# A two-layer diffusion block: low weight parts moved to VectorE, stages of the second attention layer dealt over two cycles, weight splits pinned

## The chip, the cores and the metric

The kernel runs on one core of one Trainium2 chip. The metric is the time of one execution on the device, in microseconds (us). Several executions are timed, and one more is recorded by the profiler, which gives the start and length of every instruction on TensorE (PE for its matmuls, PEld for its weight loads), VectorE (DVE), ScalarE (ACT), GpSimd (POOL) and SyncE (SP, which here only issues DMAs).

## The reference

Two trunk layers over 512 latent tokens and 256 context tokens, width 1024, in float32. Layer 0 mixes tokens by differential attention (8 heads, two maps of 64 channels each, QK-norm, rotary embedding), layer 1 by neighbourhood attention (16 heads, a learned position bias in a window, plus all context tokens). Each mixer is followed by an MLP with 4096 hidden units. Cut to what matters:

```python
for i in range(2):
    h_l = modulate(rms_norm(x, norm1_g[i]), mod_l[0], mod_l[1])
    h_c = modulate(rms_norm(ctx, norm1_g[i]), mod_c[0], mod_c[1])
    # layer 0: softmax(q0 k0) - lam * softmax(q1 k1), times v; rms_norm; times w_o
    # layer 1: softmax([q k_window + bias, q k_ctx]) times v; times w_o
    y_l, y_c = mixer(h_l, h_c, ...)
    x = x + mod_l[2] * y_l
    x = x + mod_l[5] * squared_relu_mlp(modulate(rms_norm(x, norm2_g[i]), ...), w_mlp1[i], w_mlp2[i])
    # the same for ctx in layer 0; layer 1 needs the latent tokens alone
return x
```

## The kernel before

Every float32 operand of a large matmul is split into a high part (rounded by a copy on ACT) and a low part (the operand minus the high part, a subtraction on DVE or POOL), and a product is three passes: high by high, high by low, low by high. So each weight piece needs a DMA into one of two raw buffers (tile R, line 129, `wraw`), a copy on ACT (line 145) and a subtraction (line 146, both in `wsplit`). A raw buffer is free again when both have read it. In the MLPs and in layer 0's attention the subtraction is on POOL; in layer 1's attention it is on DVE, because `split` passes `eng=nc.vector`.

Each attention layer is a software pipeline over heads (layer 0, 8 of them) or pairs of heads (layer 1, 8 groups), written out as a list of words that `run` executes in order. A word is a kind and a number; a prime means the head before the current one, two primes the one before that:

- `w`k issues the DMA of weight piece k of the next head, `c`k splits it. Four pieces make a head.
- `Q`i`a`, `Q`i`b` are the two halves (over the contraction) of the projection of token tile i to q, k and v; in layer 1 `Qi` of tiles 0 and 1 (context, no q) is one step. After the last half the accumulator (PSUM tag A) is emptied: raw q and k into a Y tile (line 412), v into its high and low parts (465 and 466 in layer 0, 619 and 620 in layer 1), squares and their sums (416, 418), a power on POOL (293), and in layer 0 the rotation (470 to 480), on POOL except for three tiles of head 0.
- `U`i transposes two tiles of q and k (496 in layer 0; 633 and 635 in layer 1) and splits them (430 to 447).
- `S`i are scores and softmax (514 to 526; 655 to 669), `T`i transposes the probabilities and splits them (538 to 541; 685 to 687), `V`i multiplies by v (549; 700) and `O`i transposes the output (566).
- `m` and `n` are pieces of the modulation, `x`, `X`, `P`, `B` belong to the output projection: fetch a head's output from DRAM (737), split it (742, 743), one half of one tile of the projection (749), and the start with weight piece 3 and the gates.

`CYCLE0`, `START0` and `END0` are layer 0's lists, `CYCLE1`, `LAST1` and `END1` layer 1's. In these stretches PE, SP and POOL keep the order in which the instructions are emitted (`PINNED`). ACT and DVE do not: at build time a scheduler with its own estimate of times sorts their instructions, so a split whose DMA it takes as landed can stand ahead of work that was emitted earlier. On the chip each engine then runs its own list strictly in order.

PSUM banks set further order. In layer 1, `PS_ATTN1` gives three banks for A, three for scores (S) and two for B, which T (two of them) and V (one) share. In layer 0, `PS_ATTN0` gives one bank for transposes (C), two for B, two for A and one set of three for scores. Of SBUF tiles, Y has six buffers, E (probabilities), X and R two, N four; H has eight, four for each group in layer 1.

## Time and profile before

| | |
|---|---|
| median of 3 runs | 1918.09 us (1917.07 to 1920.08) |
| the profiled execution's own time | 1917.39 us |
| its span | 1915.6 us |
| PE busy | 1796.2 us, 94% of the span |
| DVE, ACT, POOL busy | 1132.3, 834.9, 808.8 us |
| granted TensorE clock over the span | 0.979 |

The span is the stretch from the first to the last instruction that the profiler recorded; the time of the execution holds a little more. Busy time is the union of an engine's instructions. The granted clock is the share of full TensorE speed that the chip allowed: below 1.00 the same matmuls take longer. In a row of the timeline the columns are start, length, engine, line, operation, the tile written and the tiles read, shapes and count; square brackets hold the time for which the engine had stood idle before, and what ended that. In a row of waits stand who waited, for whom, the total, the number of times and the longest.

### The profile page before, as it was taken

The page shows a single profiled execution, that of the slowest core. Times are in us where ns is not written, and L with a number is a line of the kernel's source. Part 1 is how long each engine was busy: PE and PEld are TensorE (multiplying, and loading weights), DVE is VectorE, ACT ScalarE, POOL GpSimd, SP SyncE. Part 2 cuts the span into 40 slices and gives each one's busy share as a digit, 9 for nine tenths or more (in the row PEclk, how much of TensorE's full clock was granted, in tenths as well). Part 3 has the DMA queues.
Part 4 walks back from the last instruction along what each step waited for, and adds up shares of the span by engine and source line. Part 5 has one row for each costly group of instructions (what it writes and reads, how often), then busy time and mean ns, then how long its engine had stood idle before and what let it go on. Part 6 is the DMA issues. An engine that isn't in the chain of part 4 may idle for free.

```text
span 1915.6 us, 27143 instructions
## 1 busy us (share of the span) xinstructions
PE 1796.2 (94%) x10256; PEld 1572.7 (82%) x10256; DVE 1132.3 (59%) x2158; ACT 834.9 (44%) x1854; POOL 808.8 (42%) x688
## 2 busy tenths in 40 slices
PE   6789999997999999999999998998997989999998
PEld 5777888885789888888888978898887878888886
DVE  4478877887664343343344686777676664444447
ACT  4476666675342212212221245666677342232321
POOL 3555565653333424333342533333345444344443
PEclk9899999998999999999999999999998999999999
DMA  8122212225324443443441232112202323223332
GB/s 326 35 89 79 68 65 84 86 86 189 115 73 146 138 139 126 150 165 110 165 153 46 67 106 71 56 59 77 86 29 88 116 81 105 90 88 100 99 99 77
DMA packets 66499, 197.61 MB, mean 103 GB/s; under 512 B 8192, under 2 KB 23488, under 8 KB 60224
## 3 DMA queue, kind: packets, MB, share of 16 engines
q1 hardware_dynamic: 58608, 186.03, 29.4%
q10 hardware_dynamic: 7760, 9.85, 1.5%
q8 instruction: 80, 1.31, 0.3%
q14 instruction: 51, 0.42, 0.1%
HBM read 180.74 MB, written 15.11 MB: 102 GB/s over the span
## 4 chain that ended last, share of the span: by engine, by line
PE 71%; DVE 12%; ACT 5%; DMA 5%; issue 4%; POOL 3%; ACTq 0%; SPq 0%; POOLq 0%; DVEq 0%
PE PD L829 22%; PE PA L405 11%; PE PA L864 11%; PE PB L864 9%; PE PA L749 4%; PE PB L700 2%; PE PA L254 2%; PE PS L514 2%; PE PB L549 1%; DMA R<-in_wqa_dram 1%; DMA R<-in_wqb_dram 1%; PE PS L655 1%; ACT E L520 1%; PE PQ L395 1%; ACT W L145 1%
## 5 line engine op out<-in xcount | busy, mean ns | idle before, releaser
L146 POOL TENSOR_TENSOR W<-R,W 128x1024 fp32r<-128x1024 f32 x142 | 351.4, 2485 | 541.2 <-ACT W L145 541.1
L829 PE MATMUL PD<-Q,W 128*128 128x384 f32 (+2 forms) x1992 | 395.8, 345 | 2.4 <-DVE Q L331 1.1
L145 ACT ACTIVATE W<-R 128x1024 fp32r<-128x1024 f32 (+1 forms) x172 | 172.4, 1021 | 462.3 <-PE PA L864 193.5
L829 PEld LDWEIGHTS PD<-Q,W 128*128 128x128 f32 x1992 | 345.2, 188 | 34.0 <-issue 8.6
L864 PE MATMUL PA<-W,H 128*128 128x512 f32 x1080 | 275.5, 394 | 4.6 <-POOL W L146 2.9
L864 PEld LDWEIGHTS PA<-W,H 128*128 128x128 f32 x1080 | 200.2, 188 | 51.5 <-issue 4.5
L838 DVE TENSOR_TENSOR N<-N 128x768 f32<-128x768 f32 (+1 forms) x64 | 67.0, 1048 | 278.8 <-ACT N L834 170.3
L864 PE MATMUL PB<-W,H 128*128 128x512 f32 x840 | 209.3, 391 | 0.0
L864 PEld LDWEIGHTS PB<-W,H 128*128 128x128 f32 x840 | 157.4, 188 | 33.3
L405 PE MATMUL PA<-W,Q 128*128 128x384 f32 (+1 forms) x1008 | 172.4, 323 | 4.2 <-DVE H L620 3.8
L405 PEld LDWEIGHTS PA<-W,Q 128*128 128x128 f32 x1008 | 157.1, 189 | 6.1 <-DVE H L620 5.5
L293 POOL TENSOR_TENSOR SQ<-SQ,half 128x4 f32<-128x4 f32 (+1 forms) x96 | 93.9, 979 | 132.6 <-DVE SQ L418 131.7
L405 PE MATMUL PA<-WB,H 128*128 128x384 f32 x576 | 110.5, 344 | 9.9 <-DVE Q L466 9.9
L841 DVE SCALAR_TENSOR_TENSOR H<-N,H 128x768 fp32r<-128x768 f32 (+1 forms) x64 | 98.1, 1533 | 25.7 <-ACT H L840 25.0
L405 PEld LDWEIGHTS PA<-WB,H 128*128 128x128 f32 x576 | 100.5, 191 | 11.0 <-DVE Q L466 10.5
L749 PE MATMUL PA<-W,H 128*128 128x512 f32 x384 | 98.6, 409 | 5.6 <-POOL H L743 3.1
L829 PE MATMUL PD<-H,W 128*128 128x512 f32 (+1 forms) x408 | 94.4, 379 | 2.5 <-DVE SA L287 2.0
L875 DVE TENSOR_TENSOR H<-PA,H 128x512 f32<-128x512 f32 x78 | 53.9, 690 | 69.6 <-PE PA L864 69.6
L749 PEld LDWEIGHTS PA<-W,H 128*128 128x128 f32 x384 | 73.3, 196 | 23.9 <-POOL H L743 3.9
L829 PEld LDWEIGHTS PD<-H,W 128*128 128x128 f32 x408 | 74.0, 189 | 18.0 <-DVE H L331 2.9
L514 PE MATMUL PS<-Q,Q 128*128 128x256 f32 (+1 forms) x320 | 68.6, 346 | 18.3 <-ACT E L520 10.0
L520 ACT ACTIVATE E<-PS,SA 128x768 f32<-128x768 f32 (+1 forms) x96 | 72.7, 758 | 27.9 <-DVE SA L519 25.5
(208 smaller groups left out, 3064.4 us busy)
## 6 DMA issues: line engine op xcount, KB each, us to landing
R<-in_w_dram SPq DMA_DIRECT2D x128, 512.0 KB
M<-in_wmod_dram SPq DMA_DIRECT2D x48, 1024.0 KB
R<-in_wqa_dram SPq DMA_DIRECT2D x32, 384.0 KB
R<-in_wqb_dram SPq DMA_DIRECT2D x32, 384.0 KB
Y<-in_rpb_dram SPq DMA_DIRECT2D x48, 128.0 KB
bias<-Y SPq DMA_DIRECT2D x48, 128.0 KB
X<-bias SPq DMA_DIRECT2D x8, 768.0 KB
R<-in_woa_dram SPq DMA_DIRECT2D x8, 512.0 KB
```

The costliest lines, as they stand in the source:

```text
L145: nc.scalar.activation(w[:, 0, :n], raw, AF.Copy)
L146: low = (eng or nc.gpsimd).tensor_sub(w[:, 1, :n], raw, w[:, 0, :n].bitcast(F32))
L293: nc.gpsimd.tensor_tensor(r, ss, self.half[:, :n], op=ALU.pow)
L405: nc.tensor.matmul(acc[:, :n], hT[kt][:, x, P * i:P * i + P], w[kt // 2][:, y, o:o + n], start=(kt == 0 and p == 0), stop=(kt == KT - 1 an ...
L514: nc.tensor.matmul(s[:, c0:c1], q[:, m, P * i:P * i + P], k[:, m, c0:c1], start=p == 0, stop=p == 1)
L520: nc.scalar.activation(e[:, m, :nk], s, AF.Exp, bias=mx[:, 0:1], accum_out=sm[:, m:m + 1])
L749: nc.tensor.matmul(ps, oHL[h][:, x, c:c + P], w[h // 2][:, y, 512 * (h % 2):512 * (h % 2) + 512], start=(first and h == hs[0] and p == 0), ...
L829: nc.tensor.matmul(ps[:, at:at + b1 - b0], w[kt // 4][:, x, o:o + P], hT[kt][:, y, b0:b1], start=(kt == 0 and p == 0), stop=(kt == KT - 1 ...
L838: nc.vector.tensor_mul(r, r, r)
L841: nc.vector.scalar_tensor_tensor(u[:, 1, :], r, 1.0, u[:, 0, :].bitcast(F32), op0=ALU.mult, op1=ALU.subtract)
L864: nc.tensor.matmul(ps, hd[:, x, P * i - c0:P * i - c0 + P], w[f][:, y, 512 * n:512 * n + 512], start=(f == 0 and p == 0), stop=(f == len(h ...
L875: nc.vector.tensor_add(av, ps, av)
```

## The change

1. In layer 0's attention the subtraction of `wsplit` goes to DVE (`eng=nc.vector`) for heads 2 to 7. Heads 0 and 1 are loaded through other calls and stay on POOL.
2. The copy and the subtraction of the weight splits in both attention layers, and of the split `X` in the output projection, are given to `keep_in_program_order`: at build time each is tied behind the instruction that was emitted just before it on its engine, so the scheduler can't sort it ahead of that.
3. `c3` moves in `CYCLE0` from before `Q2a` to after `V1'`. `END0` deals its `X` and `P` steps out anew.
4. In layer 1, `T3`, `V2` and `V3` of a group move into the cycle after next, among the first steps (`T3''`, `V2''`, `V3''`), `V1` to the end of the next; `Q0` and `Q1` become two halves each; `U0` moves up; `c1 w3` moves down. `LAST1` and `END1` follow.
5. Head 0's second rotation buffer comes from the tag OT (two buffers) and no longer from Y.

```diff
-CYCLE0 = """w0 w1 Q0a O2'' n1' S1' O3'' V4'' V5'' c0 w2 U4' Q0b c1 w3 Q1a T0' T1' Q1b c2 O4'' S2' V0' c3 Q2a O5'' Q2b
-S3' T2' U0 Q3a V1' O0' Q3b S4' T3' Q4a Q4b V2' O1' m0 S5' T4' U2 n0 Q5a V3' Q5b m1 S0 T5'"""
+CYCLE0 = """w0 w1 Q0a O2'' n1' S1' O3'' V4'' V5'' c0 w2 U4' Q0b c1 w3 Q1a T0' T1' Q1b c2 O4'' S2' V0' Q2a O5'' Q2b
+S3' T2' U0 Q3a V1' c3 O0' Q3b S4' T3' Q4a Q4b V2' O1' m0 S5' T4' U2 n0 Q5a V3' Q5b m1 S0 T5'"""
...
-END0 = """x0 x1 x2 x3 S1' O2'' O3'' V4'' T0' U4' n1' V5'' T1' X0 S2' X1 O4'' x4 X2 x5 P0a O5'' V0' S3' X3 T2' X4 B0
-X5 P0b P1a V1' O0' S4' m0 P1b V2' O1' x6 P2a T3' n0 P2b T4' S5' P3a O2' P3b V3' V4' m1 T5' P4a O3' n1 X6
-P4b V5' P5a P5b O4' O5'"""
-CYCLE1 = """w0 w1 Q0 U4' Q1 c0 w2 S0' Q2a S1' c1 w3 Q2b Q3a T0' Q3b S2' T1' Q4a S3' V0' Q4b V1' Q5a c2 T2' Q5b c3 T3'
-V2' U0 U2 V3'"""
-LAST1 = """Q0 U4' Q1 c0 x0 x1 S0' Q2a S1' Q2b X0 x2 Q3a T0' Q3b X1 x3 S2' T1' Q4a S3' V0' X2 Q4b V1' Q5a T2' Q5b T3'
-V2' U0 U2 V3'"""
-END1 = """c1 X3 x4 U4' S0' S1' x5 T0' S2' X4 c2 T1' P2a V0' S3' X5 P3a B0 V1' P4a T2' V2' x6 P2b T3' X6 P3b V3' P4b
-P5a P5b"""
+END0 = """x0 x1 x2 x3 S1' O2'' O3'' V4'' T0' U4' n1' X0 V5'' T1' X1 S2' O4'' X2 x4 V0' S3' x5 P0a O5'' T2' X3 P1a
+X4 V1' O0' S4' X5 B0 P0b m0 V2' O1' x6 P1b T3' n0 P2a T4' S5' P2b O2' P3a V3' V4' P3b m1 T5' P4a O3' n1
+X6 P4b V5' P5a P5b O4' O5'"""
+CYCLE1 = """w0 w1 Q0a T3'' U4' Q1a c0 w2 V2'' V3'' Q0b S0' Q1b Q2a S1' Q2b Q3a T0' S2' Q4a c1 w3 T1' Q3b S3' V0' U0
+Q4b Q5a c2 T2' Q5b c3 U2 V1'"""
+LAST1 = """Q0a T3'' U4' Q1a c0 x0 x1 V2'' V3'' Q0b S0' Q1b X0 x2 Q2a S1' Q2b X1 Q3a T0' S2' Q4a T1' Q3b X2 S3' V0'
+U0 Q4b Q5a T2' Q5b U2 V1'"""
+END1 = """x3 x4 T3'' c1 U4' V2'' V3'' S0' X3 x5 P2a S1' c2 X4 P3a T0' S2' X5 T1' P4a B0 S3' V0' V1' P2b T2' x6 P3b
+T3' V2' X6 P4b V3' P5a P5b"""
...
-    def wsplit(self, raw, n, tile=None, eng=None, tag='W'):
+    def wsplit(self, raw, n, tile=None, eng=None, tag='W', pinned=False):
...
-        nc.scalar.activation(w[:, 0, :n], raw, AF.Copy)
+        high = nc.scalar.activation(w[:, 0, :n], raw, AF.Copy)
         low = (eng or nc.gpsimd).tensor_sub(w[:, 1, :n], raw, w[:, 0, :n].bitcast(F32))
+        if pinned:
+            self.tc.keep_in_program_order(high)
+            self.tc.keep_in_program_order(low)
...
             else:
-                t2 = self.sbt('Y', [P, 2, 2, 64])
+                t2 = self.sbt('OT' if accs else 'Y', [P, 2, 2, 64])
...
-            for hf in (0, 1) if i < 2 else (half,):
-                self.qkv_matmul(acc[i], hf, w, hT, i, c0, 384 - c0)
-            if half == 1 or i < 2:
+            self.qkv_matmul(acc[i], half, w, hT, i, c0, 384 - c0)
+            if half == 1:
...
-            nc.scalar.activation(u[:, 0, :], st, AF.Copy)
-            eng.tensor_sub(u[:, 1, :], st, u[:, 0, :].bitcast(F32))
+            self.tc.keep_in_program_order(nc.scalar.activation(u[:, 0, :], st, AF.Copy))
+            self.tc.keep_in_program_order(eng.tensor_sub(u[:, 1, :], st, u[:, 0, :].bitcast(F32)))
...
-                    w.setdefault(h, []).append(b.wsplit(raws.pop((h, k)), 768, tag=("WA", "WB")[h % 2]))
+                    w.setdefault(h, []).append(b.wsplit(raws.pop((h, k)), 768, eng=nc.vector, tag=("WA", "WB")[h % 2], pinned=True))
...
-                    w.setdefault(g, []).append(b.wsplit(raws.pop((g, k)), 768, eng=nc.vector, tag="W1"))
+                    w.setdefault(g, []).append(b.wsplit(raws.pop((g, k)), 768, eng=nc.vector, tag="W1", pinned=True))
```

## The prediction, before the change was built

> **What bounds it now.** First the page's head, then busy times by stage, then PE's waits in each stage, last the order of instructions around each wait.
>
> ```profile
> span 1915.6 us, 27143 instructions
> PE 1796.2 (94%) x10256; PEld 1572.7 (82%) x10256; DVE 1132.3 (59%) x2158; ACT 834.9 (44%) x1854; POOL 808.8 (42%) x688
> ```
>
> PE is the bound, and 119 us of the span are without it. The windows (columns: length, then busy of PE, PEld, DVE, ACT, POOL, granted clock, DMA share, GB/s) show where the change can reach:
>
> ```profile
> 67.00:205.00 138.00, 118.15 (x749) 104.72 (x750) 104.33 (x250) 88.37 (x259) 78.34 (x98) 0.96 0.20 68
> 205.00:405.00 200.00, 187.76 (x1287) 172.75 (x1286) 159.58 (x370) 137.71 (x395) 118.41 (x151) 1.00 0.24 83
> 405.00:513.00 108.00, 94.63 (x554) 76.71 (x552) 81.54 (x159) 59.48 (x157) 43.65 (x47) 0.95 0.39 137
> 1157.70:1199.40 41.70, 39.59 (x249) 38.65 (x250) 27.07 (x69) 22.77 (x64) 16.15 (x21) 0.96 0.12 39
> 1199.40:1411.10 211.70, 193.42 (x1292) 187.86 (x1291) 151.72 (x351) 143.23 (x350) 74.46 (x91) 0.94 0.19 63
> 1411.10:1453.00 41.90, 37.95 (x265) 36.49 (x264) 29.91 (x71) 30.27 (x74) 20.59 (x22) 1.00 0.18 58
> 1453.00:1506.00 53.00, 42.76 (x234) 37.82 (x233) 30.81 (x67) 32.78 (x73) 26.43 (x23) 0.81 0.35 119
> ```
>
> The rows are START0, four CYCLE0 passes, END0 with its tail, then layer 1's attention in four pieces; the fifth holds five periods of 42.3 us. PE idles 19.9, 12.2, 13.4, 2.1, 18.3, 4.0 and 10.2 us in them. Where the clock is under 1.00, matmuls also run slower: 265 in 37.95 us at clock 1.00 make 143 ns each, so 1292 would be 185.0 us instead of 193.42, a further 8.4 us in the five periods. The rest of the kernel (both MLPs, the handovers) has the same program afterwards.
>
> PE's waits (total, times, longest), first START0, then the CYCLE0 passes, END0, and the five periods of layer 1:
>
> ```profile
> PE PA L405 <- DVE Q L466: 9.9, 2, 8.6
> ...
> PE PB L538 <- DVE E L526: 4.8, 4, 1.6
> PE PS L514 <- ACT E L520: 4.3, 4, 1.3
> PE PS L514 <- ACT Q L443: 2.0, 4, 0.8
> ...
> PE PS L514 <- ACT Q L443: 4.2, 2, 2.6
> PE PA L749 <- POOL H L743: 3.1, 2, 2.2
> ...
> PE PB L700 <- DVE N L687: 13.6, 5, 2.8
> ```
>
> **The low parts and the pins, layer 0.** One pass; the first line is from the chain of waits (start, length), the others from the timeline:
>
> ```profile
> 303.21 3.38 DMA R<-in_wqa_dram
> ...
> 301.35 1.84 POOL L146 TENSOR_TENSOR WA<-R,WA 128x768 fp32r<-128x768 f32 x1
> 306.62 0.84 ACT L145 ACTIVATE WA<-R 128x768 fp32r<-128x768 f32 x1 [1.13 <-DMA R<-in_wqa_dram]
> 307.37 0.88 ACT L520 ACTIVATE E<-PS,SA 128x768 f32<-128x768 f32 x1
> 307.78 1.82 POOL L146 TENSOR_TENSOR WA<-R,WA 128x768 fp32r<-128x768 f32 x1
> 308.39 1.68 PE L514 MATMUL PS<-Q,Q 128*128 128x512 f32 x8 [1.20 <-ACT E L520]
> 308.37 0.17 DVE L523 RECIPROCAL SA<-SA 128x2 f32<-128x2 f32 x1 [2.76 <-ACT E L520]
> 308.77 0.98 DVE L558 SCALAR_TENSOR_TENSOR O<-O,SO,one 128x128 f32<-128x128 f32 x1
> ```
>
> The fourth weight piece of the pass is fetched only when a low part on POOL has freed one of two R buffers (301.35 + 1.84); it takes 3.38 us, and its high part c3 has been sorted ahead of the second exponential on ACT, waits 1.13 us for the DMA, and the exponential and PE wait behind it. The other row to see is L558: 0.98 us while POOL's low part runs (307.78 to 309.60), where L553 of the same shape takes 0.35 on average (below). It sits in front of L526, for which PE waits next.
>
> The change moves 24 low parts (heads 2 to 7, four each) from POOL to DVE:
>
> ```profile
> L146 POOL TENSOR_TENSOR WA<-R,WA x16: 1809/1825/1847, 23.2 to 307.8; 128x768 fp32r<-128x768 f32 x16
> L146 DVE TENSOR_TENSOR W<-R,W x24: 947/958/960, 1157.9 to 1417.6; 128x768 fp32r<-128x768 f32 x24
> L558 DVE SCALAR_TENSOR_TENSOR O<-O,SO,one 128x128 f32<-128x128 f32 x24 | 14.5, 606 | 0.6 <-POOL SO L293 0.3
> L553 DVE SCALAR_TENSOR_TENSOR O<-PB,SA,O 128x128 f32<-128x128 f32 x23 | 8.0, 347 | 3.1 <-ACT O L552 2.6
> ```
>
> POOL loses 24 x 1.83 = 44 us, DVE gains 24 x 0.96 = 23 us. Of those, 14 fall into 205 to 405: 13.4 us, less what L558 no longer loses, 24 x (606 - 347) ns = 6.2 us. DVE goes from 159.6 to about 167 of some 192 us. R is freed about 2 us earlier (POOL reached that low part only after other work, and needs 0.87 us more for it). SP then issues w2 and w3 earlier; nothing else queues between them but the M and oT fetches. c3 moves from before Q2a to after V1': ten steps later, so its DMA of 3.4 us has landed. w3 itself stays; only the next pass's w1 waits for c3's buffer, and that is not asked for until the next pass begins. I expect the 1.20 us before the scores and most of the L526 waits to go: of 11.1 us, I take 8. Bounds: all 12.2 gained, or 13.4 lost if every low part lies on the path.
>
> **START0.** The second buffer of the rotation moves from Y (6 buffers) to OT for head 0.
>
> ```profile
> 82.92 0.38 ACT L412 ACTIVATE Y<-PA 128x256 f32<-128x256 f32 x1 [4.74 <-DVE Y L480]
> 85.38 2.93 PE L405 MATMUL PA<-WB,H 128*128 128x384 f32 x8 [8.55 <-DVE Q L466]
> ```
>
> ACT could not empty head 1's first accumulator because no Y was free until a rotation ended (L480); PE lost 8.55 us. With Y free after U0'' (the transposes before 76.8) this wait should all but go. DVE, at 104 of 138 us, then takes head 0's remaining rotations at the same time as head 1's work, plus ten low parts (9.6 us). So I take 5 us, bounds 8.6 + 3 gained and 9.6 lost.
>
> **END0.** The fetched head outputs are split (X) and the projection's steps (P) are dealt out anew; the x4, x5, x6 DMAs keep their order on SP, ahead of B0's weight and gate fetches as before.
>
> ```profile
> 445.80 0.83 ACT L742 ACTIVATE H<-N 128x768 fp32r<-128x768 f32 x1
> 449.29 0.84 ACT L742 ACTIVATE H<-N 128x768 fp32r<-128x768 f32 x1 [1.03 <-DMA N<-oT]
> ```
>
> These are splits sorted ahead of the q and k copies (L441, L443) for which the scores wait 4.2 us; pins hold each behind what was emitted before it, and P1a now fills PE before S4. POOL's low part of X3 is emitted before P1a, no longer directly before P0b's use. Half of 13.4 idle: 6 us. Bounds 13 gained, 4 lost (two POOL parts of 1.8 us met again elsewhere).
>
> **Layer 1.** The wait that comes back every period:
>
> ```profile
> 1207.67 1.24 PE L685 MATMUL PB<-ident,E 128*128 128x128 f32 x8
> 1208.73 0.84 ACT L145 ACTIVATE W<-R 128x768 fp32r<-128x768 f32 x1 [0.31 <-DMA R<-in_wqb_dram]
> 1209.79 1.06 ACT L686 ACTIVATE N<-PB 128x512 fp32r<-128x512 f32 x2
> 1210.82 1.28 DVE L687 TENSOR_TENSOR N<-PB,N 128x512 fp32r<-128x512 f32 x2
> 1211.55 1.22 PE L700 MATMUL PB<-N,H 128*128 128x256 f32 x8 [2.64 <-DVE N L687]
> ```
>
> T3 fills both PB banks, V2 stands directly behind it and needs one; the next group's c0 is sorted ahead of T3's copies. PE stands 2.64 us, and the clock is 0.94 over the five periods, where the last piece without such long waits has 1.00. Afterwards U4' and Q1a lie between T3'' and V2'', c0 is pinned behind U4's work, and V3'' lies behind V2'':
>
> ```profile
> 1219.96 3.12 PE L405 MATMUL PA<-W,Q 128*128 128x256 f32 x24 [0.33 <-ACT H L443]
> 1201.42 1.05 PE L700 MATMUL PB<-N,H 128*128 128x256 f32 x8
> ```
>
> Q1a is half of the 24: 1.56 us, with four transposes of U4' (half of 1.24) about 2.1. T3's first bank needs one ACT copy (0.53) and one DVE subtraction (0.64), 1.2 us: covered. The second needs 1.8 us and has V2'' (1.4) more. U4' to S0' was Q1, 3.1 us; now Q1a, V2'', V3'' and Q0b, about 5.9 (2 x 1.56 + 2 x 1.4; a V is the eight of 1.05 and two narrower). c1 and w3 move past T0', S2' and Q4a: on SP w3 now stands nearer the bias fetch of U0, still with Q3b, Q4b, Q5a and Q5b (2.3 us each, 1.56 x 384 / 256) before c3, against a DMA of 3.4. POOL has no split here. The gain has a row each: 18.3 idle and 8.4 of clock, 26.7 us; I take 20. Bounds 26.7 gained, nothing gained if each wait returns elsewhere.
>
> Outside the five periods: the first piece and 1411 to 1453 idle 6.1 us, I take 3. In 1453 to 1506 PE idles 10.2 and the clock costs up to 0.19 x 42.76 = 8 us; END1 now has V2'' and V3'' between U4' and S0', P2a and P3a between the scores and T0'. On the other hand T3'', V2'', V3'' come after the last Q and P2a needs c1's piece sooner (SP issues it behind x3 and x4, long before). I take 7, bounds 18 gained, 5 lost (one DMA uncovered).
>
> **What is late next.** U2's splits stand ahead of V1's copies, and T3''s second bank needs V1's: I estimate a fifth of the old 2.7 us in six periods, +3. In layer 0 one low part a pass will stand in front of a maximum that an exponential waits for, 0.96 us in five passes, +5.
>
> **The lock between DVE and POOL.** The row is L558, 0.98 us, ending 0.15 us after POOL's subtraction. [...] The row of 24 on DVE, 947 to 960 ns beside POOL at 35%, shows no such stretch, and the sum goes by the row.
>
> **Sum.** -5 - 8 - 6 - 20 - 3 - 7 + 3 + 5 = -41 us. The profiled execution took 1917.39 us (span 1915.6), 0.7 under the median of 1918.09; 1917.4 - 41 = 1876.
>
> **Rivals.**
> 1. Layer 0 gives its gain back: DVE at 87% delays as much as the freed ACT wins; START0, the passes and END0 (5 + 8 + 6 = 19 us) bring nothing. For it: DVE is the busiest engine behind PE there, and PE's waits name it. Against it: in the pass shown DVE itself idled 2.76 us while ACT waited (L523). 1876 + 19 = 1895.
> 2. The V2 wait returns one step later: T3's copies sort behind U4's ten splits, and V3'' or S0' waits 2.7 us a period, the clock falling again. 20 + 3 lost: 1899. Against it: T3'' is emitted and ready before U4'.
> 3. All named waits go: 8.6 + 11.1 + 7.3 + 26.7 + 6 = 60 us, 1858. Against it: each stage has a second engine at 70% or more.
> 4. Slower: each low part holds DVE's queue for itself and for a POOL power that it meets:
>
> ```profile
> L293 POOL TENSOR_TENSOR SQ<-SQ,half 128x4 f32<-128x4 f32 x24 | 24.3, 1013 | 9.3 <-DVE SQ L418 9.2
> ```
>
>    0.96 + 1.01 = 1.97 us, 24 times 47 us, with the passes' 8 not won and instead of the 5: 1876 + 8 + 47 - 5 = 1926. Slower than before begins at (41 - 8 + 5) / 24 = 1.6 us for each low part. PE has slack of its own there (187.8 of 200 busy), which speaks against it.
> 5. The pins do nothing that the sorting does not undo, and the order costs what it wins: 1917.
>
> **Chances.** Forecast (1866 to 1888) 0.48; rival 1 0.17, rival 2 0.12, rival 3 0.11, rival 4 0.07, rival 5 0.05. The range 1856 to 1908 holds the first three and most of the third rival, over 0.8. A difference of 0.2% (3.8 us) is about what this measurement can tell: faster 0.87, same 0.05, slower 0.08.
>
> **What the new profile would show.** Right: in layer 1 no wait of L700 for L687 over 0.5 us, periods near 38.5 us and a clock of 0.98 or more; in layer 0 L558 near 0.35 us, no L145 before L520 waiting for a DMA, passes near 48 us; no 8.5 us hole at 77 us; POOL's L146 down by 24. Wrong: waits of L514 or L538 for DVE growing with DVE near 90%, waits of L655 for L442 to L445, or a split on ACT idle for a DMA.

## The result and the profile after

The changed kernel takes 1909.38 us in the median (1907.54 to 1911.04, four runs) where the kernel before takes 1919.09 (1917.07 to 1920.60, four runs on the same chip): a ratio of 0.995 with an interval of 0.9933 to 0.9967. It is faster, by 9.7 us and not by 41, and lies just above the predicted range, which ended at 1908. The profiled execution took 1911.04 us, against 1917.39 for that of the kernel before; the two spans differ by 6.3 us, and this is what the stages below add up to.

The head of the page after, to be held against that of before:

```profile
span 1909.3 us, 27134 instructions
PE 1797.7 (94%) x10256; PEld 1576.3 (83%) x10256; DVE 1139.6 (60%) x2182; ACT 830.6 (44%) x1854; POOL 777.5 (41%) x664
```

The 24 subtractions went from POOL to DVE as announced (688 to 664, 2158 to 2182), and PE, with the same matmuls, is busy 1.5 us longer than before: what the kernel gained is idle time of PE. To see where time went, both kernels are cut where the first projection of a head or group begins, so that a row holds the same work on both sides. The rows are START0, the four full passes, END0, layer 1's attention and its end piece; first before, then after (columns as in the prediction: length, busy of PE, PEld, DVE, ACT, POOL, granted clock, DMA share, GB/s):

```profile
67.80:183.90 116.10, 98.43 (x627) 86.45 (x627) 88.57 (x212) 73.08 (x214) 67.15 (x84) 0.96 0.16 56
183.90:387.00 203.10, 190.93 (x1305) 175.49 (x1303) 160.20 (x372) 139.33 (x401) 120.93 (x153) 1.00 0.24 82
387.00:549.40 162.40, 147.26 (x828) 122.06 (x826) 116.78 (x242) 85.03 (x223) 59.20 (x64) 0.97 0.33 114
1130.30:1424.70 294.40, 268.21 (x1767) 258.54 (x1766) 210.78 (x503) 193.99 (x477) 96.81 (x118) 0.95 0.20 67
1424.70:1541.70 117.00, 103.91 (x572) 91.71 (x572) 75.40 (x152) 65.89 (x149) 57.91 (x50) 0.91 0.27 87
```

```profile
67.20:179.60 112.40, 100.34 (x627) 88.88 (x627) 93.22 (x220) 73.95 (x215) 56.26 (x76) 0.95 0.18 58
179.60:385.20 205.60, 196.19 (x1304) 181.06 (x1303) 161.85 (x386) 139.07 (x400) 94.27 (x137) 0.97 0.25 80
385.20:556.10 170.90, 150.16 (x829) 123.84 (x827) 115.31 (x243) 85.56 (x224) 60.27 (x63) 0.93 0.31 109
1137.00:1419.70 282.70, 260.37 (x1739) 252.94 (x1738) 208.12 (x497) 187.28 (x473) 101.70 (x118) 0.96 0.20 67
1419.70:1534.70 115.00, 103.18 (x601) 90.86 (x601) 80.76 (x158) 67.66 (x153) 58.53 (x49) 0.97 0.28 95
```

The first column behind the window is the one to read. START0 gained 3.7 us, the passes lost 2.5, END0 lost 8.5, layer 1 gained 11.7 and its end piece 2.0: a sum of -6.4. The last two belong together, because matmuls of the last group moved from the one to the other (1767 to 1739, 572 to 601): -13.7. Layer 1 moved as intended, by half as much; layer 0 as a whole got slower. The clock column says that part of this isn't waiting: in the passes PE is busy 5.3 us longer for the same matmuls, at a clock of 0.97 and no longer 1.00.

**Layer 1.** PE's waits over the whole attention of layer 1, after (total, times, longest):

```profile
PE PA L408 <- ACT H L446: 9.6, 6, 1.7
PE PA L634 <- DVE Y L423: 6.3, 6, 2.8
```

The wait of V2 for T3's copies (13.6 us in five periods before) is gone, and V3'' and S0' did not inherit it. In its place Q1a's projection (L408) waits 1.6 us in every period for a copy on ACT. One period of the timeline after:

```profile
1217.40 0.14 PEld L634 LDWEIGHTS PA<-ident,Y 128*128 128x128 f32 x1
...
1218.21 0.85 ACT L145 ACTIVATE W<-R 128x768 fp32r<-128x768 f32 x1
...
1223.10 0.33 PE L634 MATMUL PA<-ident,Y 128*128 128x128 f32 x1 [0.70 <-DVE Y L423]
...
1224.70 0.38 ACT L446 ACTIVATE H<-PA 64x256 fp32r<-64x256 f32 x1
...
1225.13 2.93 PE L408 MATMUL PA<-W,Q 128*128 128x256 f32 x12 [1.59 <-ACT H L446]
```

U2's transposes begin at 1217.40 and its last copy out of PSUM ends at 1225.08, because ACT and DVE deal with c3 (1218.21), V1's and T3's copies in between. Q1a doesn't read what U2 wrote. It needs an accumulator, and of three A banks in rotation the next one is U2's: U2, Q0a, U4' and Q1a ask for one each, in this order. Besides the wait, look at the length of the last row: 2.93 us for twelve matmuls, where Q0a needs 1.64 for the same number and shape. Behind the same two waits of 0.70 and 1.59 us these twelve took 2.93, 2.62, 2.21, 1.71 and 2.93 us in the five periods from 1219 us on; the last section holds two of them against the clock records.

**The passes of layer 0.** PE's longest wait after, and a timeline around the longest wait of a pass:

```profile
PE PS L517 <- ACT Q L446: 7.6, 4, 2.1
```

```profile
292.12 0.95 DVE L146 TENSOR_TENSOR WA<-R,WA 128x768 fp32r<-128x768 f32 x1
...
293.77 0.95 DVE L146 TENSOR_TENSOR WA<-R,WA 128x768 fp32r<-128x768 f32 x1
...
297.36 0.84 ACT L145 ACTIVATE WA<-R 128x768 fp32r<-128x768 f32 x1
...
298.79 0.38 ACT L446 ACTIVATE Q<-PC 64x256 fp32r<-64x256 f32 x1
299.22 0.50 PE L517 MATMUL PS<-Q,Q 128*128 128x512 f32 x1 [1.73 <-ACT Q L446]
300.04 0.80 PE L517 MATMUL PS<-Q,Q 128*128 128x512 f32 x1 [0.32 <-DVE Q L448]
...
301.49 3.10 PE L408 MATMUL PA<-WB,H 128*128 128x384 f32 x12
```

The waits that the prediction wanted gone are gone: the old ones for the second exponential and for L526 (4.3 and 4.8 us) are no longer among the first, no split waits for a DMA, and the scaling that a POOL subtraction used to stretch to 0.98 us has one length in the passes:

```profile
L561 DVE SCALAR_TENSOR_TENSOR O<-O,SO,one x23: 342/351/353, 188.3 to 380.9; 128x128 f32<-128x128 f32 x23
```

Instead S2' waits for the last copies of U4'. These copies and subtractions alternate between ACT and DVE, six on each; two low parts on DVE (c0 and c1, at 292.12 and 293.77), and c2's copy on ACT at 297.36, stand between them.

**END0.** The longest wait there, 5.09 us, in the timeline after:

```profile
467.86 2.34 POOL L146 TENSOR_TENSOR W<-R,W 128x1024 fp32r<-128x1024 f32 x1
467.93 2.42 DVE L561 SCALAR_TENSOR_TENSOR O<-O,SO,one 128x128 f32<-128x128 f32 x1 [0.46 <-POOL SO L296]
...
470.28 0.94 DVE L522 TENSOR_REDUCE SA<-PS 128x1 f32<-128x768 f32 x1
471.26 0.90 ACT L523 ACTIVATE E<-PS,SA 128x768 f32<-128x768 f32 x1 [2.75 <-DVE SA L522]
...
472.15 0.83 ACT L743 ACTIVATE H<-N 128x768 fp32r<-128x768 f32 x1
...
473.03 1.22 PE L750 MATMUL PA<-W,H 128*128 128x512 f32 x2 [5.09 <-ACT H L743]
```

Read it from below. P0b needs the split X5. The row of its copy (472.15) shows no wait for data; the pin holds it behind S4's second exponential, which waits for a maximum, which waits for the scaling L561, which POOL's subtraction stretches from 0.35 to 2.42 us. The two rows end 0.15 us apart (467.86 + 2.34 = 470.20; 467.93 + 2.42 = 470.35). So do all the others of this kind: of the 96 scalings in the traces of before (L558) and after (L561), the 13 that began while POOL subtracted a low part took 0.98 to 2.42 us and ended 0.15 us behind it, and the other 83 took 0.33 to 0.36 us.

### The profile page after: what moved, and what is told of

Same layout as the page of the kernel before. It is cut to its first block, busy times and chain, and to the rows that moved or that the text cites. A ratio compares the mean times of both kernels' runs of the same rounds, so it can differ in the third digit from the quotient of the medians.

```text
span 1909.3 us, 27134 instructions
## 1 busy us (share of the span) xinstructions
PE 1797.7 (94%) x10256; PEld 1576.3 (83%) x10256; DVE 1139.6 (60%) x2182; ACT 830.6 (44%) x1854; POOL 777.5 (41%) x664
## 3 DMA queue, kind: packets, MB, share of 16 engines
q8 instruction: 80, 1.31, 0.3%
## 4 chain that ended last, share of the span: by engine, by line
PE 75%; DVE 13%; ACT 5%; issue 3%; POOL 2%; DMA 2%; ACTq 0%; SPq 0%; POOLq 0%; DVEq 0%
PE PD L830 22%; PE PA L408 15%; PE PA L865 11%; PE PB L865 9%; PE PA L750 4%; PE PA L257 2%; PE PS L517 2%; PE PB L552 2%; PE PS L656 2%; PE PB L701 1%; PE PQ L398 1%; DVE SA L522 1%; PE PB L686 1%; ACT E L523 1%; PE PB L541 1%
## 5 line engine op out<-in xcount | busy, mean ns | idle before, releaser
L839 DVE TENSOR_TENSOR N<-N 128x768 f32<-128x768 f32 (+1 forms) x64 | 66.9, 1047 | 279.5 <-ACT N L835 170.3
L865 PE MATMUL PB<-W,H 128*128 128x512 f32 x840 | 209.2, 391 | 0.0
L408 PE MATMUL PA<-W,Q 128*128 128x384 f32 (+1 forms) x1008 | 177.9, 331 | 11.2 <-ACT H L446 11.2
L408 PEld LDWEIGHTS PA<-W,Q 128*128 128x128 f32 x1008 | 163.5, 197 | 12.9 <-ACT H L446 12.9
L296 POOL TENSOR_TENSOR SQ<-SQ,half 128x4 f32<-128x4 f32 (+1 forms) x96 | 98.5, 1027 | 161.5 <-DVE SQ L421 158.5
L842 DVE SCALAR_TENSOR_TENSOR H<-N,H 128x768 fp32r<-128x768 f32 (+1 forms) x64 | 98.1, 1533 | 25.7 <-ACT H L841 25.0
L408 PE MATMUL PA<-WB,H 128*128 128x384 f32 x576 | 112.2, 348 | 0.8 <-DVE Q L469 0.8
L750 PE MATMUL PA<-W,H 128*128 128x512 f32 x384 | 98.4, 407 | 7.9 <-ACT H L743 5.1
L408 PEld LDWEIGHTS PA<-WB,H 128*128 128x128 f32 x576 | 102.6, 195 | 1.8 <-DVE Q L469 1.1
L876 DVE TENSOR_TENSOR H<-PA,H 128x512 f32<-128x512 f32 x78 | 53.8, 690 | 69.6 <-PE PA L865 69.6
L750 PEld LDWEIGHTS PA<-W,H 128*128 128x128 f32 x384 | 73.0, 195 | 26.0 <-ACT H L743 5.4
L517 PE MATMUL PS<-Q,Q 128*128 128x256 f32 (+1 forms) x320 | 72.1, 358 | 22.9 <-ACT Q L446 13.1
```

Source lines behind the costliest of these rows:

```text
L296: nc.gpsimd.tensor_tensor(r, ss, self.half[:, :n], op=ALU.pow)
L408: nc.tensor.matmul(acc[:, :n], hT[kt][:, x, P * i:P * i + P], w[kt // 2][:, y, o:o + n], start=(kt == 0 and p == 0), stop=(kt == KT - 1 an ...
L517: nc.tensor.matmul(s[:, c0:c1], q[:, m, P * i:P * i + P], k[:, m, c0:c1], start=p == 0, stop=p == 1)
L750: nc.tensor.matmul(ps, oHL[h][:, x, c:c + P], w[h // 2][:, y, 512 * (h % 2):512 * (h % 2) + 512], start=(first and h == hs[0] and p == 0), ...
L839: nc.vector.tensor_mul(r, r, r)
L842: nc.vector.scalar_tensor_tensor(u[:, 1, :], r, 1.0, u[:, 0, :].bitcast(F32), op0=ALU.mult, op1=ALU.subtract)
```

## The experiments

All are compared with the kernel before on the same chip. Most are single executions with a profile, and the kernel before alone went from 1910.8 to 1919.4 in nine executions on one chip. So the stage lengths, which repeat better, carry the readings. Six kernels with the same program up to layer 1 (changed, e6, e7, e9, e14, e18) spread over 2.2 us in START0, 1.2 in the passes and 0.7 in END0. Four that share all of layer 1 (changed, e1, e2, e4) spread over 0.9 us in its attention, but over 5.7 in its end piece (114.8 to 120.5), so differences in the last column are given for the attention alone where it matters. The lengths are taken from the start of the first projection of each head, as in the rows above. "Passes" is the sum of the four, "L1" layer 1's attention with its end piece. "X free" means that the splits X are not pinned; this holds for the end piece of layer 1 as well, which shares the code.

| kernel | us | before, same chip | START0 | passes | END0 | L1 |
|---|---|---|---|---|---|---|
| before | 1919.09 | | 116.1 | 203.1 | 162.4 | 411.4 |
| changed | 1909.38 | 1919.09 | 112.4 | 205.6 | 170.9 | 397.7 |
| e1, layer 0's low parts on POOL | 1904.63 | 1914.66 | 111.6 | 197.3 | 170.3 | 401.7 |
| e2, layer 0's splits not pinned | 1916.99 | 1914.66 | 112.7 | 204.9 | 171.3 | 402.7 |
| e3, before with OT alone | 1905.94 | 1914.66 | 108.6 | 203.0 | 161.2 | 409.5 |
| e4, old END0 | 1909.16 | 1914.66 | 110.3 | 204.5 | 173.3 | 398.0 |
| e5, splits X free | 1909.52 | 1914.99 | 112.6 | 206.1 | 165.9 | 402.1 |
| e6, layer 1's splits not pinned | 1926.73 | 1914.99 | 112.3 | 205.6 | 171.4 | 413.5 |
| e7, U2 earlier | 1920.25 | 1914.99 | 112.1 | 204.4 | 171.2 | 408.8 |
| e9, layer 1's old order, pinned | 1920.87 | 1914.99 | 111.0 | 204.5 | 171.3 | 410.8 |
| e10, two low parts on DVE, c3 later | 1911.87 | 1916.02 | 111.5 | 209.2 | 164.6 | 401.5 |
| e11, low parts on POOL unpinned, X free, old END0 | 1903.88 | 1916.02 | 110.1 | 202.4 | 163.9 | 401.2 |
| e13, e11 with the pins of layer 0 | 1899.43 | 1913.46 | 111.6 | 197.3 | 164.5 | 401.3 |
| e14, changed with four A banks | 1892.13 | 1913.46 | 110.2 | 204.6 | 171.6 | 381.1 |
| e16, before with four A banks | 1924.29 | 1915.98 | 116.5 | 203.4 | 163.6 | 415.6 |
| e18, e6 with four A banks | 1896.98 | 1915.98 | 111.5 | 204.6 | 171.4 | 384.6 |
| e17, e13 with four A banks | 1878.95 | 1915.98 | 112.4 | 197.3 | 164.4 | 380.6 |

### Layer 0: the low parts and their pins (e1, e2, e10, e11)

e1 keeps everything of the change but the engine of layer 0's low parts:

```diff
-b.wsplit(raws.pop((h, k)), 768, eng=nc.vector, tag=("WA", "WB")[h % 2], pinned=True)
+b.wsplit(raws.pop((h, k)), 768, tag=("WA", "WB")[h % 2], pinned=True)
```

> The changed kernel with layer 0's 24 low parts back on POOL; the pins and every order stay. The passes of layer 0 took 50.8 us instead of 50.0, with a wait of 2 us for the k copies of U4' before the scores of S2'. Theory A (the low parts of c0 and c1 on VectorE stand inside U4's chain of copies and subtractions): that wait falls to 0.8 us or less and the passes to 50 us or less. Theory B (the pinned copy of c2 on ScalarE stands before U4's last copy, wherever the low part runs): the wait stays at 1.5 to 2 us and the passes at 50.5 us or more.

The passes fall to 49.8 us for the first and 49.2 for each of the others, 197.3 together, 8.3 below the changed kernel and 5.8 below the one before. The window of the passes and the same wait of S2' as above, with the matmuls behind it, in e1:

```profile
177.90:375.20 197.30, 190.55 (x1305) 175.68 (x1303) 155.97 (x371) 138.72 (x400) 118.42 (x152) 1.00 0.25 84
```

```profile
293.05 0.96 PE L517 MATMUL PS<-Q,Q 128*128 128x512 f32 x2 [1.14 <-ACT Q L446]
...
294.32 2.25 PE L408 MATMUL PA<-WB,H 128*128 128x384 f32 x12
```

The wait is 1.14 and no longer 1.73 + 0.32 us, the clock is back at 1.00, and the twelve matmuls behind it take 2.25 us, not 3.10. The passes are thus those of theory A, while the wait lies between the two theories. Of the 8.3 us PE's busy time makes 5.6 (196.19 - 190.55) and waiting 2.7: what the low parts on DVE cost is two thirds clock. The clock records hold four stretches of 3.4 us at half clock in these passes of the changed kernel, and none in those of e1.

The two timelines also show where the 0.9 us of waiting comes from. c0's low part costs nothing more, since in e1 POOL's subtraction of c0 stretches a scaling (L561) at the same place to 1.93 us. c1's delays the subtraction L445, which begins 1.40 us after the start of the copy before it and not 0.53. The rest is no low part: the square (L419) and its sum (L421) were sorted ahead of the last copy and the last subtraction, some 0.35 us each.

e2 leaves them on DVE and drops only the pins:

```diff
-eng=nc.vector, tag=("WA", "WB")[h % 2], pinned=True
+eng=nc.vector, tag=("WA", "WB")[h % 2]
```

> The changed kernel with layer 0's weight splits on VectorE but not pinned. Theory A (low parts on VectorE are the cause): the wait of S2' for U4's copies stays near 2 us and the passes near 50.8 us. Theory B (the pin of c2's copy is the cause): the wait falls under 1 us and the passes to 49 us or less, because c3's move and the earlier freed buffers remain. If splits are sorted ahead of work again and wait for DMAs, a wait of ScalarE for the weight DMA comes back.

204.9 us: with the low parts on DVE the pins make no difference to the length of the passes. But the wait did not stay near 2 us, as theory A had it:

```profile
PE PS L517 <- ACT Q L446: 5.0, 4, 1.2
```

It is nearly as short as in e1, and PE's transposes of O (L569) wait for another subtraction on DVE (L544) instead, 2.2 us in four times. Behind 0.43 and 1.24 us the twelve matmuls took 3.51 us, and the clock between 184 and 387 us is 0.97. So the low parts on DVE cost the same by two ways, and the copies of U4' are only one of them. (The total is above the changed kernel's mostly because the end piece of layer 1, untouched here, took 120.5 us and not 115.0; more on that below.)

e10 asks which low parts hurt, and tries two more things: c0 and c1 go back to POOL, c2 and c3 stay on DVE; X is free; and in layer 1 `c3` moves over the border of the cycle.

```diff
-eng=nc.vector, tag=("WA", "WB")[h % 2], pinned=True
+eng=None if k < 2 else nc.vector, tag=("WA", "WB")[h % 2], pinned=True
...
-CYCLE1 = """w0 w1 Q0a T3'' U4' Q1a c0 w2 V2'' V3'' Q0b S0' ... Q4b Q5a c2 T2' Q5b c3 U2 V1'"""
+CYCLE1 = """w0 Q0a T3'' U4' c3' w1 Q1a V2'' V3'' Q0b c0 w2 S0' ... Q4b Q5a c2 T2' Q5b U2 V1'"""
```

> Three edits in stages that are read apart, on the changed kernel with X not pinned. (1) Layer 0: the low parts of c0 and c1 on POOL, those of c2 and c3 on VectorE. Theory A (c0's and c1's low parts stand inside U4's chain): the wait of S2' falls to about 1.1 us as with all four on POOL, the clock stays at 1.00, passes 49.2 to 49.6 us. Rival (VectorE's load as a whole): about half way, passes near 50.1 us. (2) Layer 1: c3 moves over the cycle's border to behind U4' (w1 behind it, c0 behind Q0b), out of the burst in which U2's copies wait. Theory: the 1.6 us of Q1a and the 0.7 us of U4' shrink to 0.5 us together, periods 38 to 39 us. Rival (T3's, V1's, U2's and U4's copies are enough to hold Q1a): periods stay over 40 us.

The gain that both theories expected did not come: the passes took 209.2 us, more than with all four on DVE. PE's waits in the passes of e10, and in its layer 1:

```profile
PE PS L517 <- DVE Q L448: 6.0, 4, 1.6
PE PS L517 <- ACT Q L446: 5.7, 4, 1.7
```

```profile
PE PA L408 <- ACT H L446: 10.2, 5, 2.0
```

Both waits of the passes are again those of S2' for copies of U4'. The timeline shows a harm that the mixture itself makes:

```profile
298.30 1.82 POOL L146 TENSOR_TENSOR WA<-R,WA 128x768 fp32r<-128x768 f32 x1
298.76 2.17 DVE L146 TENSOR_TENSOR WA<-R,WA 128x768 fp32r<-128x768 f32 x1 [0.44 <-ACT WA L145]
...
301.44 0.80 PE L517 MATMUL PS<-Q,Q 128*128 128x512 f32 x1 [1.49 <-DVE Q L448]
```

c2's low part on DVE meets POOL's subtraction of c1 and takes 2.17 us instead of 0.96, as it does in the other passes, and the last subtraction of U4' (L448) stands behind it. So e10 does not say which low parts do the harm in the changed kernel. Moving c3 away from U2's copies did not help layer 1 either: Q1a waits longer, 2.0 us, and the projection waits another 5.6 us for weight splits (3.2 for copies, 2.4 for low parts).

e11 has the low parts on POOL without pins, X free and the old END0.

```diff
-eng=nc.vector, tag=("WA", "WB")[h % 2], pinned=True
+tag=("WA", "WB")[h % 2]
...
-self.tc.keep_in_program_order(nc.scalar.activation(u[:, 0, :], st, AF.Copy))
-self.tc.keep_in_program_order(eng.tensor_sub(u[:, 1, :], st, u[:, 0, :].bitcast(F32)))
+nc.scalar.activation(u[:, 0, :], st, AF.Copy)
+eng.tensor_sub(u[:, 1, :], st, u[:, 0, :].bitcast(F32))
```

> Layer 0's low parts on POOL and not pinned, X not pinned, END0 as before; of the layer 0 edits c3's move and the OT buffer stay, layer 1 stays as changed. (1) START0: with OT alone it took 48.8 us from head 1's to head 2's first projection, with pins and POOL 50.7, changed 52.7. Theory: pins cost it 2 us and low parts on VectorE 2 us, so 48.8 here. (2) Passes: with pins and POOL 49.2 us, before 50.2. If c3's move alone brings the us, 49.2 here; if the pins do, 50.2. (3) Head 7 to the first MLP: with X free but the new order 165.9. Theory: 162 us with the old order, the rest of the loss being P0a's new place.

The first pass took 53.8 us, the other three 49.1 to 49.9, where the kernel before has 52.2 and 50.0 to 50.4, and e1 with pins 49.8 and three times 49.2. So in the last three passes the later `c3` brings most of the gain without any pin. In the sum of the four it brings only 0.7 of 5.8 us (203.1, 202.4, 197.3), because the first pass got longer; with the low parts on POOL the pins bring the rest.

### START0: the second rotation buffer (e3)

```diff
-t2 = self.sbt('Y', [P, 2, 2, 64])
+t2 = self.sbt('OT' if accs else 'Y', [P, 2, 2, 64])
```

> The kernel before with one edit: head 0's second rotation buffer from OT. Theory: START0's whole gain (3.9 us at the third head) comes from this; the hole of 8.55 us at 77 us goes and the time falls by 3 to 6 us. Rival: the hole closes only because the pins took weight copies out of ScalarE's way and low parts off POOL; then the hole stays over 4 us and the time falls by less than 2 us.

This one line, put into the kernel before, gives 7.5 us in START0 (116.1 to 108.6) and 8.7 us in all: nearly what the whole change gave. The changed kernel, which has the line too, shows 112.4, so its other parts took 3.8 of it back. Which of them can't be told: kernels with the same list and the same splits in START0 as the changed one spread from 110.2 to 112.6 there, and those with POOL and pins (111.6 to 112.4) lie among them.

### END0: the order or the pins of X (e4, e5)

e4 puts the old END0 list back and keeps the pins; e5 keeps the new list and drops the pins of X.

```diff
-END0 = """x0 x1 x2 x3 S1' O2'' ... U4' n1' X0 V5'' T1' X1 S2' O4'' X2 x4 V0' S3' x5 P0a O5'' ...
+END0 = """x0 x1 x2 x3 S1' O2'' ... U4' n1' V5'' T1' X0 S2' X1 O4'' x4 X2 x5 P0a O5'' V0' S3' ...
```

> The changed kernel with END0 as before; pins stay. END0 and its tail lost 8.7 us with the change. Theory: 3.3 us come from P0a no longer standing between S2' and S3', and 5.1 us from X5 being pinned behind the second exponential of S4', just before P0b needs it; both belong to the new order, so 6 to 9 us come back (about 1902 us). Rival: the pins alone slow this stretch, in any order; then less than 3 us come back.

> The changed kernel with the fetched head outputs' split (X) not pinned; the new END0 stays. From head 7's first projection to the first MLP the changed kernel takes 170.9 us, the kernel before 162.4, and with the old END0 and pins it was 173.3. Theory: the pin of X behind exponentials that wait for VectorE is the cost; X5's copy moves ahead and the 5.1 us before P0b go, so this stretch takes 164 to 167 us (the 3.3 us before S3', which belong to the order, stay). Rival: the new low parts or the order alone cost it; the stretch stays over 169 us.

END0 took 173.3 us in e4 and 165.9 in e5. My first theory, that the new order leaves S3' uncovered, fell as the main cause. One entry each of PE's waits in END0, the longest of e4 and the one of e5 that matters below:

```profile
PE PA L750 <- ACT H L743: 8.1, 2, 4.8
```

```profile
PE PS L517 <- ACT E L523: 4.8, 2, 3.0
```

With pins the projection waits for a split's copy in either order; without them it never does. (With the old list and X free it waits 3.0 us for low parts on POOL, in e11 and e13 as in the kernel before.) Taking e11 as the fourth corner (old list, X free: 163.9), the pins cost 5.0 us with the new list (170.9 - 165.9) and 9.4 with the old one. What the new list costs by itself can't be told: e5 and e10, which have it with X free, took 165.9 and 164.6 us, and e11 and e13 with the old one 163.9 and 164.5. It trades waits: the 3.0 us for low parts on POOL go, and S3' waits 3.0 us in e5, 3.4 in e10, because P0a stood between S2' and S3' and no longer does. Another 1.5 us (163.9 against 162.4 before) I have not explained.

### Layer 1: order, pins or bank (e6, e7, e9, e14, e16, e18)

e6 drops the pins of layer 1's weight splits, e9 keeps them with the old lists and whole `Q0`, `Q1`.

```diff
-b.wsplit(raws.pop((g, k)), 768, eng=nc.vector, tag="W1", pinned=True)
+b.wsplit(raws.pop((g, k)), 768, eng=nc.vector, tag="W1")
```

> The changed kernel with layer 1's weight splits not pinned; the new order stays. Theory A (the new order ended the 2.7 us wait of V2): periods stay at 40 to 41 us or fall, since the splits no longer stand ahead of U2's copies, for which Q1a waits 1.6 us. Theory B (the pins ended it): splits are sorted ahead again, a wait of over 2 us on T's or V's copies comes back, periods 42 us or more.

> The changed kernel with layer 1's three lists (and the undivided Q0 and Q1) as before; the pins stay. Theory A (order): V2 still stands right behind T3 with two banks, the wait of 2.7 us becomes 1.5 to 2.5 us, periods 41 to 42 us. Theory B (pins): with c0 kept behind U4's work the wait falls under 0.5 us and periods to 39 to 40 us without any new order.

Layer 1 took 413.5 and 410.8 us, against 411.4 before and 397.7 with both: neither the order nor the pins alone bring anything. The waits over five periods, e6 and then e9 (where L702 is V's multiplication):

```profile
PE PA L408 <- ACT H L446: 17.4, 5, 3.5
```

```profile
PE PB L702 <- DVE N L689: 10.5, 5, 2.1
```

In the new order without pins Q1a's wait is 3.5 us, more than twice as long; in the old order V2's wait is still there, at 2.1.

e7 asks whether Q1a's wait goes when U2's copies begin earlier:

```diff
-Q4b Q5a c2 T2' Q5b c3 U2 V1'"""
+Q4b Q5a c2 T2' U2 Q5b c3 V1'"""
```

> The changed kernel with U2 moved ahead of Q5b and c3 in CYCLE1 and ahead of Q5b in LAST1. In the changed kernel Q1a waits 1.6 us a period for a bank that U2's last copy frees (the bursts of c2, c3, U2, V1 and T3 on ScalarE and VectorE). Theory: with U2's copies ahead of c3's, that wait falls under 0.4 us and the period from 40.4 to 38.5 to 39.5 us. Rival: the burst as a whole is the limit, and the wait moves to T3'' or U4' with periods of 40 us or more.

Q1a's wait did go, and a longer one came: U4' waits 3.0 us for its q and k.

```profile
PE PA L634 <- DVE Y L423: 15.0, 5, 3.0
```

Starting the burst of copies earlier puts it in front of the last tile's own work. I read this at the time as the burst being the limit, wherever it is put. e14 tests the other reading, that only the bank matters:

```diff
-PS_ATTN1 = dict(A=3, S=3, B=2)
+PS_ATTN1 = dict(A=4, S=2, B=2)
```

> The changed kernel with four PSUM banks for A and two for the scores in layer 1 (three and three before). Theory: what is left of the gain in layer 1 stands in Q1a's wait (1.59 us a period for ACT's last copy of U2), and that copy counts only because it frees the third A bank; with a fourth bank this wait goes, the periods come to 38.7 to 39.5 us (40.4 in the mean now), and the time falls by 5 to 10 us, to about 1901 where the kernel before takes 1916. Rival: U2's burst of copies delays whatever comes next, whichever bank it is in; then the wait of U4' for its q and k, or of the scores for the one bank less, takes its place, the periods stay between 40 and 41 us and the time within 3 us of the changed kernel's 1909, or above it.

Layer 1 falls by 16.6 us, where the theory had said 5 to 10, and the six periods from the second group on are 37.3 us long in the mean, not 39.9. The window of layer 1's attention in e14, the longest wait of its six periods, and the place of the old wait:

```profile
1134.20:1399.90 265.70, 253.41 (x1740) 246.48 (x1738) 206.01 (x497) 187.72 (x473) 101.06 (x118) 0.98 0.21 71
```

```profile
PE PA L634 <- DVE Y L423: 6.4, 6, 2.9
```

```profile
1217.51 0.33 PE L634 MATMUL PA<-ident,Y 128*128 128x128 f32 x1 [0.70 <-DVE Y L423]
...
1217.70 1.67 PE L408 MATMUL PA<-W,Q 128*128 128x256 f32 x12
```

The instructions up to this point are the same, to a hundredth, as in the changed kernel 5.6 us later, with the same 0.70 us wait of U4'. Then Q1a starts at once and takes 1.67 us, where it waited 1.59 and took 2.93: 2.85 us in this period (in that in which the twelve took 1.71 us it is 1.6). Over the attention PE's idle time falls from 22.3 to 12.3 us (282.7 - 260.37; 265.7 - 253.41), as much as Q1a's waits had been (9.6), and its busy time by another 7.0: the clock records hold 23.9 us at half clock there in the changed kernel and 10.2 in e14. Two banks were enough for the scores here: from 1176 us on PE's waits in the attention of e14 hold 0.2 us for the scores (L656), those of the changed kernel none.

e16 gives the fourth bank to the kernel before, e18 to e6.

> The kernel before with four PSUM banks for A and two for the scores in layer 1. Theory (the third A bank limits the new order, not the old one): here PE waits for a B bank in V2 (2.7 us a period), which a fourth A bank does not touch; periods stay at 42 to 43 us, the time within 3 us of the kernel before. Rival (the spare bank is worth the same in any order): periods fall by 2 to 3 us here too, the time by 15 us or more. A loss of 5 us or more would say that the old order, in which S0 and S1 stand three steps apart, needs the third bank for the scores.

> The changed kernel with layer 1's weight splits not pinned (e6, 1926.7) and with four banks for A. Without pins Q1a waited 3.5 us for ACT's copies of U2. If the pins matter only because a late copy holds the third A bank, the fourth bank makes them dispensable: periods of 37 to 38.5 us, the time 1892 to 1898. If a split that is sorted ahead delays U4's transposes as well, whose q and k are among the same copies, the wait goes over to U4' and periods stay over 40 us, the time over 1905.

In the old order the bank brings nothing, rather a loss of 4.2 us in layer 1 (415.6) and of 8.3 in all, 4.9 above the slowest of the nine runs before; V2's wait is what it was. In the new order without pins it brings 28.9 us (413.5 to 384.6). First e16, then e18:

```profile
PE PB L700 <- DVE N L687: 13.8, 5, 2.8
```

```profile
PE PS L656 <- DVE H L448: 3.7, 6, 0.6
```

So order and bank carry the gain together, 26.8 us of it (411.4 - 384.6), and the pins, which looked decisive with three banks (15.8 us between e6 and the changed kernel), are worth 3.5 with four: they had shortened a wait for a bank that needn't be there. In the attention without the end piece the three numbers are 25.7 (294.4 - 268.7), 10.7 (293.4 - 282.7) and 3.0 (268.7 - 265.7). In e16 the scores wait 9.7 us for the splits of q and k, where before they wait 3.5 (L655, six periods); why these come later with two banks for the scores stays open.

### The better half of each stage (e13, e17)

e13 is e11 with the pins of layer 0's weight splits back; e17 adds the fourth bank.

> The changed kernel with layer 0's low parts back on POOL but the pins of layer 0's weight splits kept, the old END0 list and the splits X free. The same without these pins (e11) took 1903.9, with START0 giving its first projection of head 2 at 49.0 us and passes of 49.1 to 49.9 us. If the pins of layer 0's weight splits cost time only where the low parts on POOL stand far from their emitted place, START0 takes 50.7 as in e1 and the time is 1905 to 1906; if they help the passes, these take 49.0 to 49.2 and the time is 1902 to 1904. If both, it is equal to e11's within 1 us.

> e13 (layer 0's low parts on POOL with their pins, old END0, splits X free, layer 1 as changed; 1899.4 where the kernel before took 1913.5) with four banks for A in layer 1, which took 17.2 us from the changed kernel's layer 1. The two parts lie in different stages and should add up: layer 1's attention from the first projection to the last 263.8 to 266 us, the time 1881 to 1885 where the kernel before takes 1913 to 1919, a ratio of 0.982 to 0.984. If the clock takes part of it back (the end piece took 115 us at 0.97 and 119 at 0.93 with the same gaps), 1885 to 1889.

e13's passes are e1's to a tenth (197.3) and its END0 nearly e11's (164.5), 1899.43 us, less than the 1902 that was the lowest expectation; START0, at 111.6, shows no gain from the pins. e17 takes 1878.95 us in the median of five runs (1875.69 to 1879.44) where the kernel before takes 1915.98 (1910.80 to 1919.36, nine runs): a ratio of 0.9802, interval 0.9786 to 0.9818, and again a little less than expected (1881 to 1885). The losses that were found one by one add up: the passes are e13's (197.3 us), and the attention of layer 1 takes 265.1 us where it takes 265.7 in e14.

What is still in it: START0 at 112.4 where e3 had 108.6, and END0 at 164.4 where e3 had 161.2.

## Why the prediction was wrong

Its direction held. Of its terms START0's came out nearly right; those of the passes, of END0 and of layer 1 did not. Grouped by stage, it had -5 (START0), -8 and +5 (passes), -6 (END0), and -20, -3, -7 and +3 (layer 1). Measured: -3.7, +2.5, +8.5, -13.7. The miss of 35 us is thus 1 + 5.5 + 14.5 + 13.3.

**START0** was right in mechanism and nearly in size. The 8.55 us hole is gone, and e3 shows that the buffer by itself is worth 7.5. The rest of the change took 3.8 of it back, about what the prediction had deducted for DVE's extra work; but e1, with these low parts on POOL, shows 111.6 us as well, so that DVE's work was the reason is not shown.

**The passes.** The step that failed is "I expect the 1.20 us before the scores and most of the L526 waits to go: of 11.1 us, I take 8". They went, but the gain was credited to the wrong edit and the new wait was left out. With the low parts still on POOL, `c3` later and the pins (e1) the passes gain 5.8 us; moving the low parts to DVE costs 8.3, where "late next" had +5. I looked for the low parts in front of a maximum; one of them stands between the alternating copies of U4', for which S2' waits, and without pins others delay the subtraction before O's transposes (e2). DVE was busy for 79% of the passes (161.85 of 205.6), not 87, so a crowded DVE, rival 1's account, is not what the rows show, though its result (layer 0 brings nothing) is near: here one instruction of 0.95 us in front of a step for which PE waits was enough to make a wait. The clock, which was priced for layer 1 only, made two thirds of the loss here. (`c3` moved by eight steps, not by ten; nothing hung on it.)

**END0.** The step that failed is "pins hold each behind what was emitted before it, and P1a now fills PE before S4". I counted what a pin keeps a split from overtaking, and not what it makes the split wait for: pinned in ACT's order, X5 now stands behind an exponential, and through this behind a maximum and a POOL subtraction. e4, e5 and e11 put 5 to 9 us on that. P0a I followed to its new neighbours and not away from its old ones, S2' and S3'; by e5 and e10 that cost 2 us at most. The loss of 4 that I had allowed for was too small, since it priced POOL's parts alone.

**Layer 1.** "The gain has a row each: 18.3 idle and 8.4 of clock, 26.7 us" was right as a bound for this order: with a fourth bank the periods fall from 42.3 to 37.3 us, 25 us in five of them. With three banks they took 39.8 in the mean, 12 us in five. What failed is the step after it, "What is late next", which put +3 on what takes V2's place. It asked which data T3'' would wait for, and not which bank Q1a would. The wait was Q1a's, 9.6 us over the attention, and the clock fell behind it in four of the five periods from 1219 us on. The row was quoted in the prediction: Q1 at 1219.96 waited 0.33 us for a copy of H on ACT, and I used it only for the length of Q1. By the order in which A's three banks are asked for, this was already the wait for U2's bank, and in the new order less of PE's work and more of ACT's lies between U2 and Q1a. Rival 2, that the wait comes back a step later, was right in kind but named V3'' or S0'; the wait was Q1a's, 1.6 us and not 2.7. The end piece gained 2 of 7 us here, and nothing in e1 and e2, which share it (119.2 and 120.5 us against 117.0 before).

**The prediction's signs.** No wait of L701 over 0.5 us in the periods, L558 (now L561) at 0.35 us in the passes, no split waiting for a DMA, the hole at 77 us gone, POOL's subtractions down by 24: as said. Periods of 38.5 us and passes of 48: not so, and it was the waits of L517, L408 and L750 for copies on ACT, none of them on the list of things that would make the prediction wrong, and the clock behind them, that took the time.

## What to carry to other kernels

When a wait is removed, list what the next steps in the queue need, buffers and PSUM banks as well as data, and look for rows in the old trace where such a need already shows a few tenths of a microsecond: here that wait, 0.33 us before, was the next one, 1.59 us. A pin cost whatever its predecessor in the queue waited for (5.09 us before P0b), and a low part that was cheap by its length, 0.95 us, was dear in front of a step that PE waited for. Try a change that has several parts part by part: here one line alone gave 8.7 us where the whole change gave 9.7, layer 0 lost more than it won, and a bank that the change did not touch decided whether the new order was worth 13.7 or 30.3 (11.7 or 28.7 in the attention alone).

## What the runs showed of the hardware

**What the waits cost in clock.** In the traces of before and after the clock records hold two values, 0.50 and 1.00, and all 64 changes of the clock lie on a grid of 3.41 us. Two stretches of this grid around Q1a's wait in the changed kernel, each with the stretch behind it:

```profile
1221.46:1224.88 3.42, 1.31 (x8) 0.84 (x8) 3.05 (x8) 2.65 (x7) 1.21 (x3) 1.00 0.24 93
1224.88:1228.29 3.41, 3.16 (x15) 3.16 (x16) 1.63 (x4) 1.42 (x4) 1.80 (x5) 0.50 0.00 0
...
1344.34:1347.76 3.42, 1.83 (x14) 1.60 (x15) 2.23 (x5) 2.39 (x6) 2.06 (x6) 1.00 0.02 5
1347.76:1351.17 3.41, 3.41 (x32) 3.41 (x31) 1.69 (x4) 1.93 (x5) 0.32 (x1) 1.00 0.00 0
```

The waits are the same to a hundredth, 0.70 and 1.59 us. In the first case both lie mostly in one stretch, PE is busy for 1.31 of 3.42 us, the next stretch runs at half clock, and the twelve matmuls take 2.93 us. In the second an edge lies between the waits, PE is busy for 1.83 us, the clock stays at 1.00, and the twelve take 1.71. I counted all stretches at full clock in these two traces from 60 us on. Where PE was busy for less than 40% of a stretch, the next one ran at half clock every time (22 of 22); where it was busy for 65% or more, never (0 of 977); in between, 8 times of 33. So here the same waits cost their length and, by where they lay on the grid, nothing more or 1.22 us (2.93 - 1.71) on the twelve matmuls; as an estimate, a stretch at half clock that is full of matmuls costs half of its 3.41 us, 1.7 us. In the 977 stretches PE's idle time added up to 1.2 us at most (35% of 3.41). In e1 the wait of 1.14 us cost no clock in any pass: the clock of its passes is 1.00. This is read from the traces; no run was made to test it.

**The end piece of layer 1** took 115.0 and 114.8 us in the changed kernel and e4, and 119.2 and 120.5 in e1 and e2, which differ from them only in earlier stages. Changed kernel and e1 show about the same idle time there, 11.8 and 11.7 us; PE's busy time is 103.18 us at a clock of 0.97 in the one, and 107.54 at 0.93 in the other:

```profile
1408.70:1527.90 119.20, 107.54 (x600) 94.83 (x599) 81.71 (x158) 67.54 (x153) 58.41 (x49) 0.93 0.27 92
```

The records hold 6.8 us at half clock there in the changed kernel and e4, and 17.1 in e1 and e2. That the same stage met the grid at another place fits the counts above; the rows show no other difference. Single totals that differ by less than 5 us should be read with that in mind.
